# The 32x32 transposes of a block inverse as products with the identity: TensorE and ScalarE in place of VectorE

## The chip, the cores and the metric

The kernel runs on one core of one Trainium2 chip. The metric is the device time of one execution in microseconds. Three executions of the kernel before took 1997.05, 2003.13 and 1999.79 us; their median is 1999.79 us.

## The reference

A model on 256 tokens and 256 context tokens of width 1024, in several blocks: a first mixer that puts differential attention and an RWKV recurrence in both directions side by side, a state-space mixer, a second stack of attention kinds, each followed by a feed-forward part. Blocks are scaled and shifted by modulation vectors, products of a conditioning vector with large weights. Only the first mixer matters here, and in it two pieces:

```
def wkv_scan(r, decay, k, v, kk, b, s0, reverse):
    def step(s, inp):
        r_t, w_t, k_t, v_t, kk_t, b_t = inp
        sa = jnp.einsum('bhvk,bhk->bhv', s, -kk_t)
        s = s * w_t[:, :, None, :] + sa[..., None] * b_t[:, :, None, :] + v_t[..., None] * k_t[:, :, None, :]
        return s, jnp.einsum('bhvk,bhk->bhv', s, r_t)
    s, ys = lax.scan(step, s0, xs, reverse=reverse)
...
def diff_combine(s, lam, v):
    p = jax.nn.softmax(s.astype(jnp.float32), axis=-1)
    w = p[:, :, 0] - lam * p[:, :, 1]
    return jnp.einsum('bhqk,bhkd->bhqd', w.astype(v.dtype), v)
```

The kernel computes the scan in chunks of 64 tokens, eight in all. Since `sa` of a token depends on the tokens before it in its chunk, each chunk needs the inverse of a unit lower triangular 64x64 matrix, for each of eight heads and two directions. Four chunks are inverted together, 64 matrices in one call, and there are two calls.

## The kernel before

The program is written for one core as a class, `Kern`. Every step is a Python generator that yields its estimated cost; `weave` always advances the stream that has the smallest share of its own total done, and so fixes the order in which instructions are written down. A scheduler then orders them on each engine by priority and readiness; each engine executes its own list in that order.

The stretch of interest, about 180 to 500 us, weaves three streams. `rwkv_units` is the recurrence: preparation of the chunk matrices (L1022, L1025), `inverse` for the first half of the chunks, four `unit_step`s, `inverse` for the second half, four more. `dense` is the attention (`diff_head`: scores at L938, maximum at L941, exponentials at L944, two scalings on VectorE at L947 and L948, transposes at L952, values at L958) with its projections (L457), then, once the first half's units are done, the group norm (square roots at L563 to L573 on VectorE, statistics at L1290, gate L1311, output L1318) with modulation products between (`adas`, L483, whose weights `raw<-adaw` come in by SyncE's queue into 4 buffers), and last `out_early`, the output projection's first blocks (L1349). Its weights, too, are brought by SyncE's queue; ScalarE splits them into a high part `whi` (L424) and VectorE computes the low part `wlo` (L425). The third stream, `mods`, is more modulation products. ScalarE issues the DMAs that place the context's columns (L1336, L1337).

`inverse` keeps 32 matrices for each of four partition groups g of 32: two directions, and two diagonal blocks. In `LN` a partition is a matrix's row. The inversion wants one matrix per partition, so four transposes on VectorE (L1133) turn `LN` into `L`. Then 31 steps of two VectorE operations (L1141, L1143) build the inverse `Xi`. Six more transposes turn it back: two into `ta` (L1149), four into `LN` (L1150). 64 products per round at L1157 and L1167 with copies at L1160 (VectorE) and L1170 (ScalarE) fill the off-diagonal block. The products write to PSUM tiles of the tag `ya`, of which there are two; so do the y products of the units (L1081, L1108).

Of the kernel before, what the change touches and what calls it, by code (L numbers as in the profile page):

```python
# [10 lines left out]
AF = mybir.ActivationFunctionType  # L11
# [3 lines left out]
MUL, ADD, SUB, MAX, MIN = ALU.mult, ALU.add, ALU.subtract, ALU.max, ALU.min  # L15
# [287 lines left out]
class Kern:  # L303
# [599 lines left out]
    def diff_head(self, h, q, k, v, state):  # L903
        nc, P = self.nc, self.DF
        ident = self.C('ident')
        rot = []
        shuf = list(range(16, 32)) + list(range(16))
        for i, x in enumerate((q, k)):
            r = self.tl(P, [128, T], f'rot{i}')
            t = self.tl(P, [128, T], 'rott')  # L910
# [14 lines left out]
        for lat in range(2):  # L925
            nk = 2 + 2 * lat
            wT = self.tl(P, [128, 4, T], 'wT')
            for qt in range(2):
# [17 lines left out]
                nc.vector.reciprocal(st[:, 6:8], st[:, 4:6])  # L946
                nc.vector.tensor_scalar(e[:, 1], e[:, 1], st[:, 7:8], self.nlam, op0=MUL, op1=MUL)  # L947
                nc.vector.scalar_tensor_tensor(e[:, 0], e[:, 0], st[:, 6:7], e[:, 1], op0=MUL, op1=ADD)  # L948
# [107 lines left out]
    def unit_step(self, s, px, S):  # L1056
# [53 lines left out]
        for d in range(2):  # L1110
            c = sl if d == 0 else 3 - sl
            o = self.y[s // 4][:, :, 64 * c:64 * c + 64]
            src = py.rearrange("p (j d) c -> p j d c", d=2)[:, :, d]
            if d:
                src = src[:, :, ::-1]
            if sl < 2:
                nc.vector.tensor_copy(o, src)
            else:
                nc.vector.tensor_tensor(o, src, o, ADD)
# [3 lines left out]
    def inverse(self):  # L1123
# [4 lines left out]
        G4 = [slice(32 * g, 32 * g + 32) for g in range(4)]  # L1128
        lt = [self.LN[:, d].rearrange("p j h s c -> p (j h s) c") for d in range(2)]
        L = self.tl(U, [128, 32, 32], 'L')  # L1130
        for g in range(4):
            b = 32 * (g % 2)
            nc.vector.transpose(L[G4[g]], lt[g // 2][G4[g], :, b:b + 32].rearrange("p m t -> p t m"))  # L1133
        Xi = self.tl(U, [128, 32, 32], 'Xi')
        nc.gpsimd.memset(Xi, 0.0)
        nc.gpsimd.memset(Xi.rearrange("p a b -> p (a b)")[:, 0:1024:33], 1.0)
        yield 4.0
        for i in range(31):
# [6 lines left out]
        ta = self.tl(U, [128, 32, 32], 'L')  # L1145
        for g in (0, 2, 1, 3):
            b = 32 * (g % 2)
            if not g % 2:
                nc.vector.transpose(ta[G4[g]].rearrange("p m j -> p j m"), Xi[G4[g]].rearrange("p t j -> p j t"))  # L1149
            nc.vector.transpose(lt[g // 2][G4[g], :, b:b + 32].rearrange("p m t -> p t m"), Xi[G4[g]])  # L1150
            yield 1.5
        for half in range(2):
# [1193 lines left out]
```

## Time and profile before

| | |
|---|---|
| time, median of three | 1999.79 us |
| the profiled execution's time | 1991.42 us |
| its span, first to last instruction | 1989.6 us |
| TensorE busy | 1889.9 us, 95% |
| VectorE busy | 1445.1 us, 73% |
| ScalarE busy | 966.6 us, 49% |
| mean granted TensorE clock | 0.981 |

The profile shows one execution. PE is TensorE, DVE VectorE, ACT ScalarE, POOL GpSimd. A timeline row gives start and duration in us, engine, line, operation, output<-inputs with their shapes, a count where neighbours are drawn together, and in brackets the idle time of the engine just ahead of it with what ended it. Each float32 product leaves two records, so x128 is 64 products. PEclk is the granted clock as a share of full speed. A duration is that of the profiled execution; only the total has three runs.

### The profile page before, as it was taken

What the parts mean: (1) busy time and instruction counts of PE and PEld (TensorE: products, weight loads), DVE (VectorE), ACT (ScalarE), POOL (GpSimd) and SP (SyncE); (2) the same over time, 40 slices, a digit from 0 to 9 for tenths busy, and PEclk for the clock granted to TensorE, in tenths of its full rate; (3) what the DMA queues carried; (4) which work ended last, traced back from release to release, by engine and by line L of the source; (5) the groups of instructions that cost most, each with busy time, mean ns of one, the idle gap of its engine ahead of it and who ended that gap; (6) DMA issues with size and microseconds to landing.
All of it is one profiled execution on the core that took longest, in us unless ns stands there. A gap on an engine that the chain in (4) does not pass through costs nothing.

```text
span 1989.6 us, 37077 instructions
## 1 busy us (share of the span) xinstructions
PE 1889.9 (95%) x14690; PEld 1627.2 (82%) x14690; DVE 1445.1 (73%) x3032; ACT 966.6 (49%) x1772; POOL 220.8 (11%) x341
## 2 busy tenths in 40 slices
PE   5999889979899899998999999999999999999999
PEld 3776667647798889986778888899997888999999
DVE  3775696784799854447988888666678667778984
ACT  4455233222552434344565556456674554556653
POOL 2122402201231200011000002100030000000000
PEclk8999899979999999999999999999999999999999
DMA  7355724543388843332222224456654434356664
GB/s 297 111 187 184 233 75 128 170 138 108 116 282 241 281 169 96 96 99 74 86 74 81 83 82 144 147 180 181 186 165 155 145 106 128 119 167 183 193 191 147
DMA packets 87019, 299.78 MB, mean 151 GB/s; under 512 B 11213, under 2 KB 14685, under 8 KB 86846
## 3 DMA queue, kind: packets, MB, share of 16 engines
q1 hardware_dynamic: 62064, 221.29, 35.6%
q0 software_dynamic: 20736, 69.64, 10.7%
q10 hardware_dynamic: 4046, 6.49, 1.0%
q8 instruction: 115, 1.88, 0.4%
q14 instruction: 58, 0.48, 0.1%
HBM read 281.63 MB, written 18.90 MB: 151 GB/s over the span
## 4 chain that ended last, share of the span: by engine, by line
PE 82%; DVE 6%; DMA 4%; issue 4%; ACT 2%; POOL 1%; POOLq 0%; DVEq 0%; SPq 0%; ACTq 0%
PE psmm L457 22%; PE psmm L432 11%; PE psmm L435 11%; PE psmm L433 11%; PE psy L1752 2%; PE psmm L1689 2%; PE psmm L1349 2%; DMA ar<-adat 1%; PE psw L1757 1%; DVE wlo L425 1%; PE psa L2076 1%; PE psa L435 1%; PE psa L432 1%; PE psa L433 1%; PE pso L2125 1%
## 5 line engine op out<-in xcount | busy, mean ns | idle before, releaser
L424 ACT ACTIVATE whi<-raw 128x1024 fp32r<-128x1024 f32 x374 | 394.7, 1056 | 467.9 <-PE psmm L433 241.9
L425 DVE TENSOR_TENSOR wlo<-raw,whi 128x1024 fp32r<-128x1024 f32 x374 | 453.6, 1214 | 63.3 <-ACT whi L424 35.6
L457 PE MATMUL psmm<-hhi,whi 128*128 128x256 f32 (+1 forms) x1024 | 325.1, 340 | 6.2 <-ACT whi L424 2.5
L457 PE MATMUL psmm<-hlo,whi 128*128 128x256 f32 (+1 forms) x1024 | 319.3, 334 | 1.3 <-DVE hlo L708 1.3
L432 PE MATMUL psmm<-hhi,whi 128*128 128x258 f32 (+1 forms) x944 | 230.9, 283 | 0.5 <-ACT whi L424 0.5
L433 PE MATMUL psmm<-hlo,whi 128*128 128x258 f32 (+1 forms) x944 | 230.8, 282 | 0.0
L457 PEld LDWEIGHTS psmm<-hhi,whi 128*128 128x128 f32 x1024 | 195.0, 191 | 33.9 <-issue 10.3
L457 PEld LDWEIGHTS psmm<-hlo,whi 128*128 128x128 f32 x1024 | 195.0, 190 | 22.7 <-issue 4.2
L457 PE MATMUL psmm<-hhi,wlo 128*128 128x256 f32 (+1 forms) x1024 | 208.9, 335 | 0.3 <-DVE wlo L425 0.2
L432 PEld LDWEIGHTS psmm<-hhi,whi 128*128 128x128 f32 x944 | 178.9, 190 | 2.7 <-issue 1.0
L433 PEld LDWEIGHTS psmm<-hlo,whi 128*128 128x128 f32 x944 | 179.3, 190 | 0.7 <-issue 0.6
L457 PEld LDWEIGHTS psmm<-hhi,wlo 128*128 128x128 f32 x1024 | 154.1, 189 | 22.1 <-issue 6.6
L432 PE MATMUL psmm<-hi,whi 128*128 128x512 f32 (+1 forms) x512 | 162.4, 337 | 6.2 <-ACT hi L711 6.2
L433 PE MATMUL psmm<-lo,whi 128*128 128x512 f32 (+1 forms) x512 | 161.3, 336 | 0.0
L435 PE MATMUL psmm<-hhi,wlo 128*128 128x258 f32 (+1 forms) x944 | 132.3, 282 | 0.0
L435 PEld LDWEIGHTS psmm<-hhi,wlo 128*128 128x128 f32 x944 | 121.1, 190 | 0.0
L432 PEld LDWEIGHTS psmm<-hi,whi 128*128 128x128 f32 x512 | 96.4, 189 | 17.6 <-ACT hi L711 7.7
L521 DVE SCALAR_TENSOR_TENSOR aj<-ar,cb 128x1024 f32<-128x1024 f32 x80 | 97.6, 1220 | 13.0 <-DMA ar<-adat 10.7
L433 PEld LDWEIGHTS psmm<-lo,whi 128*128 128x128 f32 x512 | 96.4, 189 | 10.3 <-DVE lo L712 0.2
L435 PE MATMUL psmm<-hi,wlo 128*128 128x512 f32 (+1 forms) x512 | 100.1, 338 | 0.0
L1429 ACT ACTIVATE r<-r,s 128x256 f32<-128x256 f32 x96 | 48.9, 510 | 86.5 <-DVE r L1428 86.1
L435 PEld LDWEIGHTS psmm<-hi,wlo 128*128 128x128 f32 x512 | 81.5, 190 | 10.5
(607 smaller groups left out, 3681.1 us busy)
## 6 DMA issues: line engine op xcount, KB each, us to landing
raw<-w SPq DMA_DIRECT2D x128, 512.0 KB, 3.6
ar<-adat POOLq DMA_DIRECT2D x56, 512.0 KB, 5.0
raw<-win SPq DMA_DIRECT2D x55, 512.0 KB, 3.5
raw<-ssdin SPq DMA_DIRECT2D x49, 512.0 KB, 3.5
raw<-hyin SPq DMA_DIRECT2D x26, 512.0 KB, 5.4
raw<-adaw SPq DMA_DIRECT2D x24, 512.0 KB, 3.9
raw<-wg SPq DMA_DIRECT2D x22, 512.0 KB, 4.2
raw<-wu SPq DMA_DIRECT2D x22, 512.0 KB, 4.3
```

The lines of the kernel that those rows point to most:

```text
L424: nc.scalar.activation(hi[:, :n], raw, AF.Copy)
L425: nc.vector.tensor_tensor(lo[:, :n], raw, hi[:, :n].bitcast(F32), SUB)
L432: nc.tensor.matmul(ps, whi[:, k], act.hi[k][:, n0:n1], start=start and i == 0, stop=False)
L433: nc.tensor.matmul(ps, whi[:, k], act.lo[k][:, n0:n1], start=False, stop=False)
L435: nc.tensor.matmul(ps, wlo[:, k], act.hi[k][:, n0:n1], start=False, stop=stop and i == len(ks) - 1)
L457: nc.tensor.matmul(ps, w[:, k], a[k][:, n0:n1], start=i == 0, stop=i == len(runs) - 1)
L521: nc.vector.scalar_tensor_tensor(junk, raw, 1.0, cb[j], op0=MUL, op1=MUL, accum_out=self.mod[l][:, b, j:j + 1])
L1349: nc.tensor.matmul(ps[:, :n], w[:, c + k], a[k], start=c + i == 0, stop=c > 0 and i == len(runs) - 1, skip_group_check=True)
L1429: nc.scalar.activation(r[:, s], r[:, s], AF.Relu, bias=sh)
L1689: nc.tensor.matmul(ps, w[:, k0 + k], a[k], start=start and i == 0, stop=stop and i == len(runs) - 1, skip_group_check=True)
L1752: nc.tensor.matmul(o, w[:, q], m[:, q], start=d == 0 and n == 2 and q < 2 and k == 0, stop=k == 1 and d == 1 and n == 3, skip_group_check= ...
L1757: nc.tensor.matmul(ph, Bt[:, i], xw.rearrange("p h c -> p (h c)"), start=n != 1, stop=n > 0)
```

## The change

Three edits. The ten VectorE transposes of each inverse go; in their place `turned` makes 16 matrix columns at a time on TensorE: for each column and each partition group a 32x32 product, with the data as stationary operand and a 32x32 block of the identity moving, into a `ya` tile, which ScalarE copies to where the transpose had written. `turned` is used three times per inverse: for L (four groups, 128 products), `upper` (groups 0 and 2, 64) and `diagonal` (four groups, 128). Second, the scaling of the second softmax becomes a small VectorE product of 128x1 and a copy with scale on ScalarE. Third, the y copies of the first two units of a half go from VectorE to ScalarE. The estimated costs that the generators yield sum to the same.

```diff
--- before.py
+++ after.py
@@ -944,7 +944,8 @@
                     nc.scalar.activation(e[:, m], pss[m], AF.Exp, scale=0.125, bias=st[:, 2 + m:3 + m],
                                          accum_out=st[:, 4 + m:5 + m])
                 nc.vector.reciprocal(st[:, 6:8], st[:, 4:6])
-                nc.vector.tensor_scalar(e[:, 1], e[:, 1], st[:, 7:8], self.nlam, op0=MUL, op1=MUL)
+                nc.vector.tensor_tensor(st[:, 7:8], st[:, 7:8], self.nlam, MUL)
+                nc.scalar.activation(e[:, 1], e[:, 1], AF.Copy, scale=st[:, 7:8])
                 nc.vector.scalar_tensor_tensor(e[:, 0], e[:, 0], st[:, 6:7], e[:, 1], op0=MUL, op1=ADD)
                 yield 2.2
                 pt = self.PSt('w')
@@ -1114,7 +1115,7 @@
             if d:
                 src = src[:, :, ::-1]
             if sl < 2:
-                nc.vector.tensor_copy(o, src)
+                nc.scalar.activation(o, src, AF.Copy)
             else:
                 nc.vector.tensor_tensor(o, src, o, ADD)
         yield 0.8 * self.C_STEP
@@ -1127,14 +1128,25 @@
         nc, U = self.nc, self.U
         G4 = [slice(32 * g, 32 * g + 32) for g in range(4)]
         lt = [self.LN[:, d].rearrange("p j h s c -> p (j h s) c") for d in range(2)]
+        ident = self.C('ident')
+
+        def turned(out, rows, groups):
+
+            for i0 in (0, 16):
+                ps = self.PSt('ya').rearrange("p (i c) -> p i c", i=16)
+                for i in range(16):
+                    for g in groups:
+                        nc.tensor.matmul(ps[G4[g], i], rows(g, i0 + i), ident[G4[g], G4[g]], start=True, stop=True)
+                out(slice(i0, i0 + 16), ps)
+                yield 1.5
+
         L = self.tl(U, [128, 32, 32], 'L')
-        for g in range(4):
-            b = 32 * (g % 2)
-            nc.vector.transpose(L[G4[g]], lt[g // 2][G4[g], :, b:b + 32].rearrange("p m t -> p t m"))
+        yield from turned(lambda i, ps: nc.scalar.activation(L[:, i], ps, AF.Copy),
+                          lambda g, t: lt[g // 2][G4[g], :, 32 * (g % 2) + t], range(4))
         Xi = self.tl(U, [128, 32, 32], 'Xi')
         nc.gpsimd.memset(Xi, 0.0)
         nc.gpsimd.memset(Xi.rearrange("p a b -> p (a b)")[:, 0:1024:33], 1.0)
-        yield 4.0
+        yield 1.0
         for i in range(31):
             n, w = 31 - i, i + 1
             tmp = self.tl(U, [128, n, w], 'itmp', bufs=2)
@@ -1143,12 +1155,19 @@
             nc.vector.tensor_tensor(Xi[:, i + 1:, :w], Xi[:, i + 1:, :w], tmp, SUB)
             yield self.C_INV
         ta = self.tl(U, [128, 32, 32], 'L')
-        for g in (0, 2, 1, 3):
-            b = 32 * (g % 2)
-            if not g % 2:
-                nc.vector.transpose(ta[G4[g]].rearrange("p m j -> p j m"), Xi[G4[g]].rearrange("p t j -> p j t"))
-            nc.vector.transpose(lt[g // 2][G4[g], :, b:b + 32].rearrange("p m t -> p t m"), Xi[G4[g]])
-            yield 1.5
+
+        def upper(j, ps):
+            for g in (0, 2):
+                nc.scalar.activation(ta[G4[g], :, j], ps[G4[g]].rearrange("p j m -> p m j"), AF.Copy)
+
+        def diagonal(t, ps):
+            for g in range(4):
+                b = 32 * (g % 2)
+                nc.scalar.activation(lt[g // 2][G4[g], :, b + t.start:b + t.stop],
+                                     ps[G4[g]].rearrange("p t m -> p m t"), AF.Copy)
+
+        yield from turned(upper, lambda g, j: Xi[G4[g], :, j], (0, 2))
+        yield from turned(diagonal, lambda g, t: Xi[G4[g], t], range(4))
         for half in range(2):
             ms = slice(16 * half, 16 * half + 16)
             ps = self.PSt('ya').rearrange("p (m j) -> p m j", m=16)
```

In the listings below each row is an instruction (or neighbours alike, with their count) in TensorE's list: line, operation, output<-inputs with tile numbers, and the output's shape. Behind the change the lines have new numbers: L952, L958, L1051, L1066, L1077, L1157, L1167 and L1349 are L953, L959, L1052, L1067, L1078, L1176, L1186 and L1368; the products with the identity are L1139.

TensorE at the head of the second inverse, from the third modulation product (`psmm_3909`) on, before:

```order
L1051 MATMUL psx_4463<-uv_3599,LN_1971 64x64
L483 MATMUL psmm_3909<-raw_3914,scc_93 32x512
L1051 MATMUL psx_4463<-uv_3599,LN_1971 64x64 x6
L1066 MATMUL psx_4463<-S_2253,ar_3597 64x128 x8
L1077 MATMUL pss_4498<-S_2253,cst_83 64x512
L483 MATMUL psmm_3909<-raw_3916,scc_93 32x512
L483 MATMUL psmm_3909<-raw_3910,scc_93 32x512
L483 MATMUL psmm_3909<-raw_3912,scc_93 32x512
L483 MATMUL psmm_3909<-raw_3914,scc_93 32x512
L483 MATMUL psmm_3909<-raw_3916,scc_93 32x512
L1077 MATMUL pss_4498<-S_2253,cst_83 64x512
L952 MATMUL psw_3752<-cst_83,e_3720 128x128 x4
```

After the change, from the first product for L on (`psya`; `cst` is the identity), which stands behind the third modulation product and five key products (L1052):

```order
L1139 MATMUL psya_4151<-cst_83,LN_1971 32x32 x64
L1139 MATMUL psya_4217<-cst_83,LN_1971 32x32 x43
L953 MATMUL psw_4098<-cst_83,e_4065 128x128 x4
L1139 MATMUL psya_4217<-cst_83,LN_1971 32x32 x21
L483 MATMUL psmm_4383<-raw_4390,scc_93 32x512
L483 MATMUL psmm_4383<-raw_4384,scc_93 32x512
L959 MATMUL psw_4104<-wT_4005,vT_3880 128x256 x4
L483 MATMUL psmm_4383<-raw_4386,scc_93 32x512
L483 MATMUL psmm_4383<-raw_4388,scc_93 32x512
L483 MATMUL psmm_4383<-raw_4390,scc_93 32x512
L1052 MATMUL psx_5139<-uv_3943,LN_1971 64x64
L1067 MATMUL psx_5139<-S_2256,ar_3941 64x128 x8
```

The products for L have come in here, and the state products (L1066, now L1067) have moved from ahead of the last head's transposes (L952, now L953) to behind its values (L959).

TensorE after the last step of the first inverse, before:

```order
L483 MATMUL psmm_2884<-raw_2891,scc_93 32x512
L1157 MATMUL psya_2665<-L_2615,LN_1971 32x32
L1157 MATMUL psya_2717<-L_2615,LN_1971 32x32
L952 MATMUL psw_2600<-cst_83,e_2566 128x128 x4
L938 MATMUL psw_2620<-df_2359,df_2210 128x256
L938 MATMUL psw_2620<-rot_2441,rot_2435 128x256
L938 MATMUL psw_2621<-df_2359,df_2210 128x256
L938 MATMUL psw_2621<-rot_2441,rot_2435 128x256
L1157 MATMUL psya_2665<-L_2615,LN_1971 32x32 x31
L1157 MATMUL psya_2717<-L_2615,LN_1971 32x32 x31
L457 MATMUL psmm_3106<-hhi_109,whi_3102 128x512
```

After the change, behind 57 of the `upper` products (`psya_2751`, `psya_2803`), which follow the same four L483 rows:

```order
L953 MATMUL psw_2735<-cst_83,e_2700 128x128 x4
L938 MATMUL psw_2788<-df_2491,df_2213 128x256
L938 MATMUL psw_2788<-rot_2573,rot_2567 128x256
L938 MATMUL psw_2789<-df_2491,df_2213 128x256
L938 MATMUL psw_2789<-rot_2573,rot_2567 128x256
L1139 MATMUL psya_2803<-cst_83,Xi_2415 32x32 x7
L1139 MATMUL psya_2846<-cst_83,Xi_2415 32x32 x64
L1139 MATMUL psya_2921<-cst_83,Xi_2415 32x32 x64
L1052 MATMUL psx_3235<-uv_2260,LN_1971 64x64 x6
L953 MATMUL psw_2915<-cst_83,e_2786 128x128 x4
L1052 MATMUL psx_3235<-uv_2260,LN_1971 64x64 x2
L1176 MATMUL psya_3003<-L_2750,LN_1971 32x32 x32
```

The projection products (L457) that followed L1157 directly now come after the whole inverse; between the diagonal products (`psya_2846`, `psya_2921`) and L1176 stand key products and four transposes.

TensorE in the tail of the second inverse, before, where the first two L1157 products stand ahead of the output projection:

```order
L491 MATMUL psw_4044<-cst_83,adas_4042 128x128 x4
L1157 MATMUL psya_4275<-L_4223,LN_1971 32x32
L1157 MATMUL psya_4331<-L_4223,LN_1971 32x32
L1349 MATMUL psmm_4114<-hhi_4051,whi_4110 128x512
L1349 MATMUL psmm_4114<-hlo_4052,whi_4110 128x512
```

The `upper` products now stand at this place. The diagonal ones come three output blocks later, after the change:

```order
L1368 MATMUL psmm_4788<-hlo_4533,whi_4784 128x512
L1368 MATMUL psmm_4788<-hhi_4536,whi_4784 128x512
L1368 MATMUL psmm_4788<-hlo_4537,whi_4784 128x512
L1139 MATMUL psya_4795<-cst_83,Xi_4316 32x32 x64
L1368 MATMUL psmm_4788<-hhi_4543,whi_4784 128x512
L1368 MATMUL psmm_4788<-hlo_4544,whi_4784 128x512
L1368 MATMUL psmm_4788<-hhi_4525,wlo_4785 128x512
L1368 MATMUL psmm_4788<-hhi_4532,wlo_4785 128x512
L1368 MATMUL psmm_4788<-hhi_4536,wlo_4785 128x512
L1368 MATMUL psmm_4788<-hhi_4543,wlo_4785 128x512
L1139 MATMUL psya_4870<-cst_83,Xi_4316 32x32 x64
```

Both sets of 64 have come between the products of one output block.

## Rows read from the trace of the kernel before

**Rows 1.** The page, parts 1 and 4: span, engines' busy time, the chain.
```profile
span 1989.6 us, 37077 instructions
...
PE 1889.9 (95%) x14690; PEld 1627.2 (82%) x14690; DVE 1445.1 (73%) x3032; ACT 966.6 (49%) x1772; POOL 220.8 (11%) x341
...
PE 82%; DVE 6%; DMA 4%; issue 4%; ACT 2%; POOL 1%; POOLq 0%; DVEq 0%; SPq 0%; ACTq 0%
```

**Rows 2.** Busy us of each engine by stretch; PEclk, DMA share, GB/s.
```profile
240.00:250.00 10.00, 10.00 (x44) 7.89 (x44) 9.90 (x11) 1.66 (x2) 0.00 (x0) 1.00 0.26 77
280.00:290.00 10.00, 6.38 (x36) 3.97 (x34) 9.55 (x18) 2.10 (x6) 0.00 (x0) 0.96 0.43 152
290.00:300.00 10.00, 10.00 (x143) 8.22 (x143) 9.75 (x11) 3.87 (x7) 0.75 (x1) 0.53 0.17 64
320.00:380.00 60.00, 59.64 (x754) 45.28 (x753) 38.41 (x91) 18.93 (x47) 18.29 (x25) 1.00 0.46 135
440.00:450.00 10.00, 9.92 (x55) 8.44 (x54) 9.83 (x11) 2.12 (x2) 0.00 (x0) 1.00 0.29 72
```

**Rows 3.** Groups of instructions by line, 180 to 500 us: busy, mean ns, idle.
```profile
L944 ACT ACTIVATE e<-psw,st 128x256 f32<-128x256 f32 (+1 forms) x32 | 18.3, 576 | 40.9 <-DVE st L942 40.9
...
L1133 DVE STREAM_TRANSPOSE L<-LN 32x1024 f32<-32x1024 f32 x8 | 15.7, 1962 | 0.2
L1150 DVE STREAM_TRANSPOSE LN<-Xi 32x1024 f32<-32x1024 f32 x8 | 15.6, 1950 | 0.1
...
L1149 DVE STREAM_TRANSPOSE L<-Xi 32x1024 f32<-32x1024 f32 x4 | 8.1, 2034 | 0.1
L947 DVE TENSOR_SCALAR e<-e,st,lam 128x256 f32<-128x256 f32 (+1 forms) x16 | 8.1, 504 | 0.2
...
L1170 ACT ACTIVATE LN<-psya 32x512 f32<-32x512 f32 x8 | 4.7, 587 | 7.3 <-PE psya L1167 7.1
```

**Rows 4.** Timeline of PE, first inverse: start, us, instruction, idle before.
```profile
253.33 0.63 PE L952 MATMUL psw<-cst,e 128*128 128x128 f32 x4 [2.80 <-DVE e L948]
...
285.79 0.31 PE L1157 MATMUL psya<-L,LN 32*32 32x32 f32 x4 [1.10 <-DVE L L1149]
288.62 0.63 PE L952 MATMUL psw<-cst,e 128*128 128x128 f32 x4 [2.53 <-DVE e L948]
...
292.00 3.62 PE L1157 MATMUL psya<-L,LN 32*32 32x32 f32 x124
295.54 0.80 PE L457 MATMUL psmm<-hhi,whi 128*128 128x512 f32 x1
...
299.12 0.54 PE L457 MATMUL psmm<-hhi,whi 128*128 128x512 f32 x1
...
300.90 0.40 PE L457 MATMUL psmm<-hlo,whi 128*128 128x512 f32 x1
```

**Rows 5.** Timeline of PE around the second inverse.
```profile
386.39 1.05 PE L483 MATMUL psmm<-raw,scc 128*32 128x512 f32 x2 [0.36 <-DMA raw<-adaw]
...
389.89 1.90 PE L483 MATMUL psmm<-raw,scc 128*32 128x512 f32 x10
...
431.79 0.42 PE L1157 MATMUL psya<-L,LN 32*32 32x32 f32 x4 [4.92 <-DVE L L1149]
432.67 0.79 PE L1349 MATMUL psmm<-hhi,whi 128*128 128x512 f32 x1 [0.46 <-ACT whi L424]
...
459.77 2.21 PE L1167 MATMUL psya<-LN,L 32*32 32x32 f32 x128
```

**Rows 6.** Timeline of DVE around the second inverse's beginning.
```profile
384.31 1.90 DVE L1133 STREAM_TRANSPOSE L<-LN 32x1024 f32<-32x1024 f32 x1
...
393.63 0.20 DVE L1141 TENSOR_TENSOR itmp<-L,Xi 128x31 f32<-128x31 f32 x1
...
398.44 0.16 DVE L563 TENSOR_SCALAR rqv<-psw 128x4 f32<-128x4 f32 x1 [0.52 <-PE psw L552]
```

**Rows 7.** Timeline of ACT before the output projection's first split.
```profile
431.56 2.00 ACT L424 ACTIVATE whi<-raw 128x1024 fp32r<-128x1024 f32 x2 [5.39 <-DMA hhi<-xT]
```

## The prediction

> **What bounds the kernel now.** I read the page first: TensorE is busy for 95% of the span and carries 82% of the chain that ended last, VectorE 73% and 6%, ScalarE 49% and 2% [rows 1]. So VectorE time that is taken away is worth something only where TensorE waits for VectorE, and every product added where TensorE is full is paid in whole. Which places are which, a table of ten-microsecond stretches over the two inverses tells [rows 2]: from 320 to 380 us TensorE is busy for 59.64 of 60 us at full clock, around 440 us for 9.92 of 10. Between 280 and 300 it is different. It is busy for only 6.38 of 10 us, and in the next ten the granted clock is 0.53, about the lower of the two levels (1.2 of 2.4 GHz). That clock follows a stretch in which the engine waited.
>
> The timeline of TensorE names the waits. Around the first inverse they are 2.80 us at 253.33 (for the softmax's last scaling on VectorE), 1.10 us at 285.79 and 2.53 us at 288.62 [rows 4]; in all three VectorE is late because 2 us transposes stand in its queue. Around the second inverse the four first transposes end near 393.6 and the 31 steps begin [rows 6], while TensorE takes modulation products as their weights arrive (0.36 us of waiting for a DMA at 386.39); at the end it waits 4.92 us for a transposed quadrant at 431.79, but the output projection's first product can't start before 432.67 anyway, since it waits for a ScalarE weight split [rows 5], and that split for the DMAs of the context's columns [rows 7].
>
> **The change, part by part.** *What goes.* Per inverse VectorE loses four transposes of 1.96 us, two of 2.03 and four of 1.95 [rows 3]: 4 x 1.96 + 2 x 2.03 + 4 x 1.95 = 19.7 us. *What comes.* Per inverse 128 + 64 + 128 = 320 products of 32x32 with the identity, 640 in all, and ScalarE gets 2 copies of 128x512 and 12 of 32x512 (0.587 us each by the eviction at L1170, 12 of them 7.0 us [rows 3]).
>
> *The price of a product.* The nearest row is L1167 in the second inverse: 128 records, two for each float32 product, in 2.21 us at full clock, so 34.5 ns for a product when two of the 32x32 quadrants alternate [rows 5]. The `upper` set has the same two quadrants: 64 x 35 = 2.2 us. The other two sets go round four quadrants. If four work at once as two do, a product costs half, 17.5 ns; the modulation products, which go to four column groups of one PSUM tile, speak for it: one alone shows 1.05 us, but ten records, five products, 1.90 us [rows 5]. If the issue of instructions or the PSUM tile is the limit, it stays 35 ns. I take 24, nearer to the row that shows four at once: 128 x 24 = 3.1 us for each set, and 2.2 + 3.1 + 3.1 = 8.4 us per inverse, with bounds 2.2 + 256 x 17.5 = 6.7 and 2.2 + 256 x 35 = 11.2.
>
> The row of the modulation products writes four column groups from full-height weights, so it doesn't show four row groups in one tile. The Trainium skill, "TensorEngine Tiling (Array Packing)", Gotcha 1 (PSUM Pressure), says that different row tiles can't access the same PSUM bank at the same time; all four quadrants here write one tile. By that rule it would be 35 ns or more and the sum that of the queued quadrants below.
>
> *First inverse.* To be had: the waits 2.80 + 1.10 + 2.53 = 6.4 us, and the low clock. At that clock 124 records took 3.62 us, 58 ns a product, 1.5 us above 62 x 34.5 ns; eight projection products from 295.54 took 3.58 us, where the next seven took 1.78 (2.0 for eight) [rows 4], another 1.5; with the rotary and transposing products before them about 4 us. Together 10.4. To be paid: 8.4 us of products, since TensorE has no gap left once the waits are gone: 240 to 250, where the products for L fall, and 320 to 380 are full [rows 2]. And new waits: the order of the changed program puts the whole tail of this inverse ahead of the projection products, with little between. From the first diagonal product to L1176 there are 64 products (1.5 us) and eight copies one after the other on ScalarE (4.7 us); beside these TensorE has the other 64 products (1.5), the key products and four transposes (about 1.0): 6.2 - 2.5 = 3.7, of which I count 2.5, since the copies of the first half start while its products still run. 8.4 + 2.5 - 10.4 = **+0.5 us**.
>
> *Second inverse, head.* The 128 products stand behind the third modulation product, which waits for its weights until 386.39 and ends at 387.4 [rows 5]; with five key products behind it they start near 387.9. 3.1 us of products, 0.55 of a softmax transpose in between and a last copy of 0.6 let the steps start at 392.1 to 392.3 instead of 393.63. That 1.3 us is worth little: the steps share VectorE with a chain that begins with the last head's square roots (398.44 [rows 6]) and runs over the group norm to the weight split. That chain's TensorE rows now stand behind 3.1 us of products, and get back the moved state products (L1066 and one L1077, about 2 us): **+1.0 us**.
>
> *Second inverse, tail.* The 4.92 us wait for the transpose goes, but the split at 431.56 ends last there, not the transpose, so its `upper` products fall into a gap: nothing. TensorE busier in the gap could lift the clock of the first eight output products; they run at 0.43 us spacing up to 435.8, and half of their excess of 1.7 us is **-0.8**. The diagonal products, 3.1 us, lie between output products in a stretch that is full (9.92 of 10 [rows 2]); VectorE's relief is worth nothing there: **+3.1**.
>
> *Softmax scale and y copies.* On VectorE 0.504 us becomes a 128x1 product (about 0.15), and ScalarE adds about 0.58 (as its exponential [rows 3]): the chain of one chunk gets 0.2 longer, sixteen times, but TensorE waits for that chain three times in the stretch [rows 4], and two of these waits go: **+0.2**. The y copies change engines with TensorE at other units' products: 0. If that cover failed, eight times the difference of two engines' copies is under 1 us.
>
> Sum: 0.5 + 1.0 - 0.8 + 3.1 + 0.2 = **+4.0 us**. The profiled execution took 1991.42 us, so it would take 1995.4; that execution lies 8.4 us below the median of the runs, 1999.79, and the same change on the median gives **2003.8 us**.
>
> Bounds: the product's price moves the sum by -3.5 (17.5 ns in both inverses, `upper` unchanged) or +5.6 (35 ns); new waits 0 to 5, so 2.5 either way; the first inverse's clock, if not regained, +4; the clock of the output products 0 to 1.7, so 0.9 either way.
>
> **The rivals.** *Faster.* Four quadrants work at once, the copies hide, and the steps start early because weights for the modulation products come sooner (they are requested when buffers come free, and everything ahead ran earlier). Then -3.5 for the price, -2.5 for the waits, -0.9 for the clock, and the head's products start at 384.3, when the last evacuation of L1025 ends and the first transpose began [rows 6], instead of 387.9: -3.6. 4.0 - 10.5 = -6.5, **1993.3 us**. For it: the 1.90 us row. Against: that the copies hide needs fillers that the order doesn't have. It decides in my favour only if diagonal products cost under 20 ns and L1176 waits under 1 us.
>
> *Slower: quadrants queue.* Every product costs 35 ns, whatever its quadrant: 4.0 + 5.6 = +9.6, **2009.4 us**. For it: L1167 already has two quadrants and yet 34.5 ns, so the instructions, not the array, may be its limit; 640 products of two records and two weight loads each are many instructions. It decides from about 28 ns on.
>
> *Slower: the strided weights.* 256 of the products for L load a stationary operand with 512 bytes between its elements, 128 of `upper` 128 bytes; no row shows such a load. If they cost two ordinary products, 70 ns, L's sets grow by 5.9 us each and `upper`'s by 2.2: +16 us, **2020 us**. Against it: weight loads lie beside products on their own queue. The Trainium skill, "SBUF — State Buffer", Specifications (TRN2), states 16-byte cachelines that want two hits each for full bandwidth; every element here is on a line of its own, and no run here shows the cost.
>
> **How the numbers follow.** Chances: my forecast 0.48, the fast case 0.20, queued quadrants 0.24, strided weights 0.08. My forecast's own range is 1997 to 2010. The range for 8 in 10 reaches from the middle of the fast case to well past that of the queued quadrants: **1993 to 2014**; left out are half of the fast case, the strided weights and an edge of the queued ones. A measurement of this kernel tells about 0.3%, 6 us, from no change. Faster by more: 0.12 of the fast case and 0.05 of mine, 0.17. Slower by more: 0.08, 0.19 of the queued ones and 0.11 of mine, 0.38. Between: 0.45.
>
> **What would show it.** In the changed profile: L1139 at 15 to 28 ns a product in the four-quadrant sets and 35 in `upper`; the waits at L953 near 253 and 288 gone, and a new one of 1 to 4 us at L1176 for ScalarE; clock 1.00 around 290; the first step of the second inverse at 1 to 2 us before its place now; output products beginning within 2 us of their old distance from the modulation products; TensorE full from there on with the diagonal products in it. I am wrong if the tail of the first inverse stands still longer than its old waits together (6.4 us), if the strided sets cost twice the others, or if the group norm's chain, not the products, carries the difference.

## The result and the profile after

The changed kernel took 2015.55 us (median of 5; 2009.12 to 2017.38), the kernel before 1998.06 us (median of 5): ratio 1.0073, 95% interval [1.0052, 1.0093], 10 to 19 us slower (the two medians lie 17.5 us apart). On the prediction's base of 1999.79 us that is 2014.4 us: at the upper edge of the range for 8 in 10, 0.4 us above it, and past the forecast's own range (to 2010), on the slower side that had 0.38. The direction of the sum was right, its size of 4.0 us was not.

The page of the changed kernel, the parts of [rows 1]:

```profile
span 2014.2 us, 39681 instructions
...
PE 1917.7 (95%) x15970; PEld 1653.6 (82%) x15970; DVE 1401.1 (70%) x3004; ACT 994.2 (49%) x1824; POOL 220.7 (11%) x341
...
PE 78%; DVE 8%; issue 4%; DMA 3%; ACT 2%; POOL 2%; ACTq 0%; POOLq 0%; DVEq 0%; SPq 0%
```

VectorE lost 44 us of busy time and TensorE gained 28. The chain has moved from TensorE to waits on VectorE and others (82% to 78%).

Busy time by stretch, columns as in [rows 2]; the last row is the second inverse's tail:

```profile
280.00:290.00 10.00, 10.00 (x160) 7.50 (x159) 4.90 (x16) 4.32 (x9) 0.00 (x0) 1.00 0.01 2
290.00:300.00 10.00, 6.75 (x364) 5.78 (x361) 3.40 (x9) 8.52 (x16) 0.75 (x1) 0.97 0.10 31
320.00:380.00 60.00, 57.00 (x700) 43.06 (x698) 32.67 (x77) 23.00 (x53) 17.17 (x23) 1.00 0.55 173
440.00:450.00 10.00, 9.44 (x126) 8.20 (x122) 2.36 (x2) 4.24 (x6) 0.00 (x0) 0.52 0.79 282
460.00:470.00 10.00, 8.29 (x307) 6.96 (x307) 1.98 (x4) 5.69 (x9) 0.00 (x0) 0.83 0.19 58
```

The stretch at 280 us is full now, as predicted. But 290 to 300 has the gap instead (6.75 of 10), 320 to 380 is 57.00 of 60 instead of 59.64, and in the tail there is a gap in a stretch that was full, with the clock at 0.83. Over 440 to 450, where the first output products lie, the granted clock is 0.52, the lower level for nearly all of the ten us.

The copies of the diagonal blocks cost 587 ns each, as was taken from L1170. In the listings below "issue" is idle time for which the profile has no releaser.

Timeline of TensorE behind the first inverse's last step (compare [rows 4]); 283.93 are products of `upper`, 293.39 the second diagonal set, L1176 the old L1157:

```profile
283.93 3.48 PE L1139 MATMUL psya<-cst,Xi 32*32 32x32 f32 x114
...
293.39 1.16 PE L1139 MATMUL psya<-cst,Xi 32*32 32x32 f32 x114 [1.42 <-issue]
...
297.12 0.38 PE L953 MATMUL psw<-cst,e 128*128 128x128 f32 x2 [1.57 <-issue]
...
297.69 1.20 PE L1176 MATMUL psya<-L,LN 32*32 32x32 f32 x64
```

57 products of `upper` took 3.48 us, 61 ns each, at full clock. The wait for ScalarE that was expected ahead of L1176 is not there; two idle times without a releaser are, 1.42 and 1.57 us.

Around the second inverse (compare [rows 5]; 395.29 answers to 386.39, 443.57 to 432.67), and the first product of the stage that follows the recurrence (L432):

```profile
395.29 1.04 PE L483 MATMUL psmm<-raw,scc 128*32 128x512 f32 x2 [0.57 <-DMA raw<-adaw]
...
396.75 3.31 PE L1139 MATMUL psya<-cst,LN 32*32 32x32 f32 x214
...
401.41 0.69 PE L1139 MATMUL psya<-cst,LN 32*32 32x32 f32 x33 [0.48 <-issue]
...
439.17 3.84 PE L1139 MATMUL psya<-cst,Xi 32*32 32x32 f32 x128 [1.36 <-DVE Xi L1155]
443.57 0.80 PE L1368 MATMUL psmm<-hhi,whi 128*128 128x512 f32 x1 [0.56 <-ACT whi L424]
...
460.55 1.29 PE L1139 MATMUL psya<-cst,Xi 32*32 32x32 f32 x128
...
463.35 1.17 PE L1139 MATMUL psya<-cst,Xi 32*32 32x32 f32 x115
466.24 0.32 PE L1139 MATMUL psya<-cst,Xi 32*32 32x32 f32 x13 [1.71 <-issue]
...
528.56 0.74 PE L432 MATMUL psmm<-zhi,whi 128*128 128x256 f32 x4 [0.58 <-ACT zhi L711]
```

107 products for L took 3.31 us, 31 ns each; the 64 of `upper` at 439.17 took 3.84, 60 ns, at a granted clock of 0.53; the 64 diagonal ones at 460.55 took 1.29, 20 ns. In the second diagonal set TensorE stops for 1.71 us behind 57 products, again without a releaser. VectorE at the head (compare [rows 6]):

```profile
402.84 0.21 DVE L1153 TENSOR_TENSOR itmp<-L,Xi 128x31 f32<-128x31 f32 x1 [5.87 <-ACT L L1144]
...
409.99 0.16 DVE L563 TENSOR_SCALAR rqv<-psw 128x4 f32<-128x4 f32 x1 [1.66 <-PE psw L552]
```

Measured from the third modulation product, the first step is 0.3 us later than before (402.84 - 395.29 = 7.55 against 7.24), the square roots 2.65 later (14.70 against 12.05), the output projection's first product 2.0 later (48.28 against 46.28).

From here on four marks divide the time: the end of the chunk products L1022 ahead of the first inverse and ahead of the second, the output projection's first product, and L432. Of the kernel before, the rows of the first two marks and that of the last:

```profile
235.85 1.68 PE L1022 MATMUL psya<-Xi,bka 64*128 64x128 f32 x16 [0.68 <-DMA Xi<-ard]
...
381.99 1.05 PE L1022 MATMUL psya<-Xi,bka 64*128 64x128 f32 x10
...
510.94 0.74 PE L432 MATMUL psmm<-zhi,whi 128*128 128x256 f32 x4 [0.58 <-ACT zhi L711]
```

With [rows 5] the last stretch, the second inverse's tail with the units of the second half, is 510.94 - 432.67 = 78.3 us; after it is 528.56 - 443.57 = **85.0**. The marks of the first stretch after:

```profile
238.41 1.71 PE L1023 MATMUL psya<-Xi,bka 64*128 64x128 f32 x16
...
391.81 0.38 PE L1023 MATMUL psya<-Xi,bka 64*128 64x128 f32 x2
```

392.19 - 240.12 = 152.1 us. Before it was 145.5 (from 237.53 to 383.04). Three kernels below have the order of the kernel before up to here, second_only, no_back and head_second; they took 146.1, 147.1 and 147.3. The marks of second_only:

```profile
238.68 3.09 PE L1022 MATMUL psya<-Xi,bka 64*128 64x128 f32 x16
...
386.86 1.05 PE L1022 MATMUL psya<-Xi,bka 64*128 64x128 f32 x10
```

So against the mean of these four, 146.5, about 5.6 us of the loss lie in the first stretch, 1.8 between marks two and three (51.4 against 49.6) and 6.7 in the last: 14.1, which agrees with the ratio's 10 to 19. Each of these lengths is that of one execution.

How the first stretch is made up, for before, after and first_only (products in the first inverse alone, below), columns as in [rows 2]; beside after, what TensorE waited for ahead of the softmax's transposes there, columns as in [rows 3]:

```profile
237.53:383.04 145.51, 138.10 (x1487) 103.76 (x1486) 113.84 (x263) 46.40 (x105) 23.49 (x32) 0.96 0.35 109
```

```profile
240.12:392.19 152.07, 144.94 (x2127) 110.85 (x2128) 91.43 (x248) 62.90 (x135) 23.48 (x32) 0.98 0.34 105
...
L953 PE MATMUL psw<-cst,e 128*128 128x128 f32 x40 | 7.2, 286 | 3.0 <-issue 1.6 <-DVE e L949 1.3
```

```profile
239.73:390.99 151.26, 149.73 (x2128) 112.58 (x2128) 95.06 (x252) 54.28 (x119) 23.50 (x32) 0.93 0.34 106
```

TensorE stands idle for 145.51 - 138.10 = 7.4 us before and 152.07 - 144.94 = 7.1 us after, although the waits that the prediction named are gone; 3.7 us of the 7.1 are stops without a releaser. The mean granted clock is 0.96 before (0.95 in the three kernels with its order) and 0.98 after. In first_only it is the other way round, 1.5 us idle and a clock of 0.93, and the stretch is about as long.

### The profile page after: what moved, and what is told of

Its sections match the earlier page's. It is cut to its first block, busy times and chain, and to the rows that moved or that the text cites. A ratio compares the mean times of both kernels' runs of the same rounds, so it can differ in the third digit from the quotient of the medians.

```text
span 2014.2 us, 39681 instructions
## 1 busy us (share of the span) xinstructions
PE 1917.7 (95%) x15970; PEld 1653.6 (82%) x15970; DVE 1401.1 (70%) x3004; ACT 994.2 (49%) x1824; POOL 220.7 (11%) x341
## 4 chain that ended last, share of the span: by engine, by line
PE 78%; DVE 8%; issue 4%; DMA 3%; ACT 2%; POOL 2%; ACTq 0%; POOLq 0%; DVEq 0%; SPq 0%
PE psmm L457 22%; PE psmm L432 11%; PE psmm L435 11%; PE psmm L433 10%; PE psy L1771 2%; PE psmm L1368 2%; DVE aj L521 2%; PE psmm L1708 2%; DMA ar<-adat 2%; DVE wlo L425 1%; PE psw L1776 1%; PE psa L2095 1%; PE psa L435 1%; PE psa L432 1%; PE psa L433 1%
## 5 line engine op out<-in xcount | busy, mean ns | idle before, releaser
L457 PE MATMUL psmm<-hhi,whi 128*128 128x256 f32 (+1 forms) x1024 | 325.4, 340 | 7.6 <-ACT whi L424 3.9
L457 PE MATMUL psmm<-hlo,whi 128*128 128x256 f32 (+1 forms) x1024 | 319.8, 334 | 1.5 <-DVE hlo L708 1.5
L432 PE MATMUL psmm<-hhi,whi 128*128 128x258 f32 (+1 forms) x944 | 231.9, 283 | 0.5 <-ACT whi L424 0.5
L457 PEld LDWEIGHTS psmm<-hhi,whi 128*128 128x128 f32 x1024 | 195.3, 191 | 34.9 <-issue 9.8
L457 PEld LDWEIGHTS psmm<-hlo,whi 128*128 128x128 f32 x1024 | 195.7, 191 | 22.6 <-DVE hlo L708 4.2
L457 PE MATMUL psmm<-hhi,wlo 128*128 128x256 f32 (+1 forms) x1024 | 209.0, 334 | 0.3 <-DVE wlo L425 0.2
L432 PEld LDWEIGHTS psmm<-hhi,whi 128*128 128x128 f32 x944 | 178.7, 189 | 2.7 <-ACT whi L424 1.6
L457 PEld LDWEIGHTS psmm<-hhi,wlo 128*128 128x128 f32 x1024 | 153.8, 189 | 22.8 <-issue 7.3
L432 PE MATMUL psmm<-hi,whi 128*128 128x512 f32 (+1 forms) x512 | 163.0, 338 | 6.3 <-ACT hi L711 6.3
L432 PEld LDWEIGHTS psmm<-hi,whi 128*128 128x128 f32 x512 | 96.5, 189 | 17.8 <-ACT hi L711 8.0
```

The source lines that it names most:

```text
L432: nc.tensor.matmul(ps, whi[:, k], act.hi[k][:, n0:n1], start=start and i == 0, stop=False)
L457: nc.tensor.matmul(ps, w[:, k], a[k][:, n0:n1], start=i == 0, stop=i == len(runs) - 1)
```

## The experiments

All times are medians, and ratios to the kernel before with their 95% intervals. L and its lines are those of the change's diff.

**Which part?** Four kernels undo the change in pieces. `transposes_only` and `scales_only`:

```diff
# transposes_only: softmax scale and y copies as before
-                nc.scalar.activation(e[:, 1], e[:, 1], AF.Copy, scale=st[:, 7:8])
+                nc.vector.tensor_scalar(e[:, 1], e[:, 1], st[:, 7:8], self.nlam, op0=MUL, op1=MUL)
...
-                nc.scalar.activation(o, src, AF.Copy)
+                nc.vector.tensor_copy(o, src)
# scales_only: all transposes on VectorE, as before
```

> The products for the transposes alone; softmax scale and y copies stay on VectorE. Theory A (the transposes carry the whole loss, about 9 us at the first inverse and about 8.5 at the second): 14 to 18 us above the kernel before, as the full change. Theory B (the copies that went to ScalarE delay its queue and carry a good part of it): at most 10 us above.

> The softmax scale and the y copies on ScalarE alone, all transposes on VectorE. Theory A: within 3 us of the kernel before, and TensorE's waits around the inverses as in the kernel before. Theory B: 5 us or more above.

transposes_only: 2010.58 us, 1.0066 [1.0051, 1.0080], 10 to 16 us above. scales_only: 2001.93 us, 1.0030 [1.0016, 1.0044], 3 to 9 above. Neither theory holds alone: the transposes carry most, but the scales are not free, as theory A and the prediction (0.2) had them. The scales lengthen the first stretch to 151.0 us and transposes_only has 151.0 too, so in the full change's 152.1 the two don't add.

`first_only` and `second_only` have products in one of the two calls of `inverse` (with `st` handed in) and VectorE's transposes in the other:

```diff
-        yield from turned(lambda i, ps: nc.scalar.activation(L[:, i], ps, AF.Copy), ...
+        if (1, 0)[st]:          # second_only: (0, 1); likewise for upper and diagonal
+            yield from turned(lambda i, ps: nc.scalar.activation(L[:, i], ps, AF.Copy), ...
+        else:
+            for g in range(4):
+                nc.vector.transpose(L[G4[g]], ...
```

> Products for the transposes in the first inverse alone, everything else as before. Theory A: 6 to 10 us above the kernel before. The prediction's term for this inverse (+0.5): within 3 us. If the 4 us by which the changed kernel is late ahead of the first inverse come from DMAs that differ from run to run, about 4 us above.

> Products for the transposes in the second inverse alone. Theory A: 7 to 10 us above (2.4 at the head, 1.2 of low clock ahead of the output products, 5.5 in the tail). The prediction's term (+3.3): 3 to 4 us. Rival C, instruction loading: the idle times of TensorE that end with no releaser appear here too, 1.4 to 1.8 us behind about 57 diagonal products of a set, at the same count of instructions although the time is another.

first_only: 2006.60 us, 1.0044 [1.0028, 1.0059], 6 to 12 us above; its first stretch took 151.3 us, its last 80.0. second_only: 2006.92 us, 1.0058 [1.0041, 1.0075], 8 to 15 above. In second_only (TensorE; L1384 is the output product, L1138 the products with the identity):

```profile
437.05 0.80 PE L1384 MATMUL psmm<-hhi,whi 128*128 128x512 f32 x1 [8.29 <-ACT whi L424]
...
450.42 2.00 PE L1138 MATMUL psya<-cst,Xi 32*32 32x32 f32 x64
...
461.84 0.37 PE L1138 MATMUL psya<-cst,Xi 32*32 32x32 f32 x19 [0.43 <-issue]
...
522.65 0.73 PE L432 MATMUL psmm<-zhi,whi 128*128 128x256 f32 x4 [0.58 <-ACT zhi L711]
```

Its last stretch is 522.65 - 437.05 = 85.6 us, as long as in the full change, but made up otherwise. Rival C's stop has the expected place, behind 54 diagonal products, and not the expected size: 0.43 us instead of 1.4 to 1.8. In its stead all of `upper` (two groups of 32 products, 2.00 us each) lies between the output products here, where after it lies ahead of the first one; with 2.6 us of diagonal products that makes 7.0 of the 7.3 us above 78.3. Both inverses lose, each more than the prediction's +0.5 and +3.3. Here `upper` ran at full clock, and 32 of its products took 2.00 us: 62 ns, about the 60 at the low clock after.

**Is it the stride of the weights?** `weights_in_rows` is the full change with the stationary operands read along rows; it multiplies other elements than the inverse needs.

```diff
-                          lambda g, t: lt[g // 2][G4[g], :, 32 * (g % 2) + t], range(4))
+                          lambda g, t: lt[g // 2][G4[g], t, 32 * (g % 2):32 * (g % 2) + 32], range(4))
...
-        yield from turned(upper, lambda g, j: Xi[G4[g], :, j], (0, 2))
+        yield from turned(upper, lambda g, j: Xi[G4[g], j], (0, 2))
```

> The full change, but the stationary operands for L and upper are read along rows (32 neighbouring elements) instead of along columns (512 or 128 bytes apart): the same number of products, of other data, so the inverse it builds is not the one that is wanted. Theory A (a strided weight load is what makes L and upper dearer than diagonal): a product of the L sets falls from 32 to about 20 ns, of upper from 61 to about 35, 3.2 us less per inverse, and the whole is 3 to 6 us below the full change, 9 to 12 above the kernel before. Theory B (the sets differ by place or clock, not by stride): prices stay at 32 and 61 ns and the time stays within 2 us of the full change.

2007.33 us, 1.0040 [1.0025, 1.0054]: about 6 us below the full change. The products for L at the head of the second inverse:

```profile
387.63 1.19 PE L1139 MATMUL psya<-cst,LN 32*32 32x32 f32 x117
391.11 1.92 PE L1139 MATMUL psya<-cst,LN 32*32 32x32 f32 x128 [2.30 <-issue]
394.84 0.42 PE L1139 MATMUL psya<-cst,LN 32*32 32x32 f32 x11 [1.81 <-issue]
```

58 products in 1.19 us are 20 ns each, where the strided ones took 31: theory A. `upper` can't be compared, since without the column order its products started between the steps; so the total isn't the price of the stride alone. But the set as a whole is not quicker: TensorE now stops for 2.30 and 1.81 us without a releaser, and 128 products that need 2.6 us take 7.6. Something other than the array limits them.

**What are the stops?** Three kernels, all on the full change: each diagonal product of the second inverse twice; the diagonal products and their copies there left out; the sets written down in quarters.

```diff
# diag_twice (second inverse alone)
-        yield from turned(diagonal, lambda g, t: Xi[G4[g], t], range(4))
+        yield from turned(diagonal, lambda g, t: Xi[G4[g], t], [0, 1, 2, 3] * (1 + st))
# no_diag
+        if st == 0:
             yield from turned(diagonal, lambda g, t: Xi[G4[g], t], range(4))
+        else:
+            yield 3.0
# spread, in turned
+                    if i % 4 == 3 and i < 15:
+                        yield 0.375
                 out(slice(i0, i0 + 16), ps)
-                yield 1.5
+                yield 0.375
```

> The full change with each diagonal product of the second inverse issued twice (same result, 128 products more, no other instruction). If the array is the limit (20 ns a product): 2.6 us above the full change, the idle time without releaser behind 57 products still 1.7 us. If the supply of instructions is the limit (theory C): 4.5 us or more above, with two or three such idle times of 1.4 us or more instead of one.

> The full change without the diagonal products and their eight copies in the second inverse (left out; the second half's units work with the blocks as they were). The prediction's term for them, 3.1 us of products in a full stretch: 3 us below the full change. Theory A with the idle time counted in: 4.3 us below; with the low clock behind it too: 5.5 to 6 us.

> The full change, but the sets of products are written down in quarters, so that other products come between them (in the second tail 16, six output products, 48, and again). Theory C (supply of instructions): the idle time of 1.7 us in the second tail falls below 0.7 and the time by 1 to 2 us. If the idle time comes from the sets themselves (PSUM tiles, quadrants): it stays, and the time is within 1 us of the full change.

diag_twice: 2021.53 us, 1.0103 [1.0085, 1.0120]. TensorE, from the first output product to L432:

```profile
442.70 0.80 PE L1368 MATMUL psmm<-hhi,whi 128*128 128x512 f32 x1 [0.56 <-ACT whi L424]
...
458.55 2.29 PE L1139 MATMUL psya<-cst,Xi 32*32 32x32 f32 x249
464.56 0.33 PE L1139 MATMUL psya<-cst,Xi 32*32 32x32 f32 x7 [3.73 <-issue]
...
467.68 3.12 PE L1139 MATMUL psya<-cst,Xi 32*32 32x32 f32 x243
472.28 0.32 PE L1139 MATMUL psya<-cst,Xi 32*32 32x32 f32 x13 [1.48 <-issue]
...
535.90 0.74 PE L432 MATMUL psmm<-zhi,whi 128*128 128x256 f32 x4 [0.58 <-ACT zhi L711]
```

By the ratios it is 6 us above the full change, with intervals that overlap. The stretch is 93.2 us, 8.2 more than after: 128 products more at 64 ns each, although 249 records ran at 18 ns a product. The stops are 3.73 and 1.48 us where there was one of 1.71, and as in theory C they come after a certain number of instructions. The instruction queue's line of the page (packets, MB, share), before, after and here:

```profile
q8 instruction: 115, 1.88, 0.4%
```

```profile
q8 instruction: 125, 2.05, 0.4%
```

```profile
q8 instruction: 127, 2.08, 0.4%
```

After the change TensorE executes 2560 instructions more than before (1280 records and as many weight loads, by the page and [rows 1]), and 10 packets more came; the 512 of diag_twice (128 products with two records and two weight loads each) came with two: one packet of 16 KB for 256 instructions, 64 products. The 2 x 15970 instructions of TensorE after make 124.8 such packets, the 2 x 14690 before 114.8, so this queue is TensorE's. A set of 64 products is one packet, executed in 1.3 us.

no_diag (2011.31 us, 1.0051 [1.0034, 1.0068]):

```profile
447.13 0.80 PE L1371 MATMUL psmm<-hhi,whi 128*128 128x512 f32 x1 [1.08 <-ACT whi L424]
...
525.71 0.74 PE L432 MATMUL psmm<-zhi,whi 128*128 128x256 f32 x4 [0.58 <-ACT zhi L711]
```

78.6 us: without the diagonal sets the last stretch is as long as before. They cost 6.4 us there: 2.5 of products, the 1.71 us stop, and 1.7 of low clock behind the stop (0.83 over 460 to 470, in the table above) make 5.9. Its total lies only 4 us below the full change, with intervals that overlap; its profiled execution had a longer low clock in the first stretch.

spread (2014.75 us, 1.0071 [1.0051, 1.0092]):

```profile
443.69 0.80 PE L1370 MATMUL psmm<-hhi,whi 128*128 128x512 f32 x1
...
465.40 0.37 PE L1139 MATMUL psya<-cst,Xi 32*32 32x32 f32 x19 [1.11 <-issue]
...
526.94 0.74 PE L432 MATMUL psmm<-zhi,whi 128*128 128x256 f32 x4 [0.58 <-ACT zhi L711]
```

The stop shrinks to 1.11 us and the stretch to 83.3, 1.7 less, between both theories; the expected 0.7 us was not reached. The total can't tell it from the full change.

The trace also shows when each packet of this queue was taken and landed. Of the kernel after, the queue in the 1 us from 463.87 on:

```profile
q8 instruction: 1, 0.02, 5.8%
```

5.8% of 16 engines for 1 us are 0.92 us, so this packet landed at 464.79. TensorE had stopped at 464.5 and went on at 466.24. The same at other stops (us):

| kernel | TensorE stops | packet begins | lands | TensorE goes on | landing to going on |
|---|---|---|---|---|---|
| after | 292.0 | 290.92 | 291.95 | 293.39 | 1.44 |
| after | 464.5 | 463.87 | 464.79 | 466.24 | 1.45 |
| second_only | 461.4 | 459.44 | 460.38 | 461.84 | 1.46 |
| weights_in_rows | 388.8 | 388.73 | 389.83 | 391.11 | 1.28 |
| diag_twice | 460.8 | 462.32 | 463.28 | 464.56 | 1.28 |
| spread | 464.3 | 462.98 | 463.86 | 465.40 | 1.54 |

In all fourteen kernels together 36 stops of 0.2 us or more without a releaser lie between 240 and 560 us, and each ends 1.2 to 1.6 us behind the landing of such a packet. In the six rows the next packet begins 1.1 to 1.2 us after TensorE goes on, so where TensorE is held up in this way the packets follow each other at some 3.5 us (290.92 and 294.49 after, 388.73 and 392.28 in weights_in_rows), 55 ns for each of 64 products. The stop that ends at 297.12 after falls between two ordinary transposes (L953), so it isn't a matter of the small products' tiles. So theory C holds: the stops are waits for instructions. What takes the time between landing and going on, the trace doesn't tell.

**Is VectorE's relief worth anything?** `no_back` is the kernel before without the four transposes back into LN in the second inverse (`if st == 0` ahead of L1150).

> The kernel before without the four transposes that put the second inverse's result back into LN (left out; the units of the second half then work with the matrices as they were): 7.8 us of VectorE fewer in the tail of the second inverse. The prediction's claim that VectorE's relief is worth nothing there: within 2 us of the kernel before, and the stretch from the first output product to the end of the recurrence as long as before (78.3 us). If relief is worth something there, 3 to 8 us below.

1998.74 us, 0.9991 [0.9980, 1.0002]:

```profile
435.61 0.80 PE L1350 MATMUL psmm<-hhi,whi 128*128 128x512 f32 x1
...
514.02 0.74 PE L432 MATMUL psmm<-zhi,whi 128*128 128x256 f32 x4 [0.58 <-ACT zhi L711]
```

78.4 us, as before. The claim holds: 7.8 us of VectorE in that tail are worth nothing that can be measured.

**Is there a better half?** `head_second` has products for L in the second inverse alone, `diag_first` for the diagonal blocks of the first alone (flags as in first_only).

> The kernel before with products for L in the second inverse alone. Theory A (the second head's gain is given back): group norm begins about 4 us earlier, and the output projection's first product waits that much longer for its DMAs, so within 2 us of the kernel before. Rival: the head's products are what makes the second inverse slow: 3 us or more above. Third: 3 to 4 us below, if the loss on the way to the output projection came from the upper products.

> The kernel before with products for the diagonal blocks of the first inverse alone (contiguous weights, 20 ns each, 2.6 us), VectorE relieved of four transposes where TensorE waits for it. Theory A (TensorE's waits of 2.5 us there go, 2.6 us of products come): within 2 us of the kernel before. If the low clock at 290 to 300 us goes with the waits: 3 to 5 us below, faster than both kernels. If small products of themselves keep the clock low: 2 to 4 us above.

head_second: 2002.07 us, 1.0012 [1.0001, 1.0024]:

```profile
434.96 0.79 PE L1384 MATMUL psmm<-hhi,whi 128*128 128x512 f32 x1 [8.28 <-ACT whi L424]
...
517.24 0.74 PE L432 MATMUL psmm<-zhi,whi 128*128 128x256 f32 x4 [0.58 <-ACT zhi L711]
```

Counted from the second mark, the group norm's first statistics product begins 3.8 us earlier, and the first output product waits 8.28 us for the split, which itself waited 7.9 us for the DMAs; a part is given back there, and the rest in the tail (82.3 us), where the transposes that follow now stand ahead of VectorE's output work: at 454.87 TensorE waits 1.57 us for it (L1390). diag_first: 1998.86 us, 1.0002 [0.9989, 1.0014]: the waits that go and the products that come are even. Neither beats the kernel before.

**Which of the scales?** `softmax_only`: the softmax scale on ScalarE, all else before.

> The kernel before with the softmax scale alone on ScalarE (y copies and transposes on VectorE). The scales alone cost about 4 us where 0.2 was predicted. If the softmax scale is the cause (its chain from the exponential to the transposes is longer and the order around it is another): 3 to 5 us above the kernel before. If the y copies are: within 1.5 us.

2002.37 us, 1.0016 [1.0002, 1.0030]: 0.4 to 6 us above. It can be half of the scales' loss or all of it; whether the y copies have a share, the intervals don't tell. The last stretch is 78.3 us in both kernels, so the loss lies ahead of it. In scales_only it shows in the first stretch (151.0 against 146.5), in softmax_only more in the next (53.0 against 49.6), each in one execution; by what mechanism stays open.

## Why the prediction came out as it did

- *What bounds the kernel, and VectorE's relief: right.* The three waits around the first inverse, 6.4 us, are gone as such; all waits for the softmax's last scaling (L949) in the first stretch add up to 1.3 us. Relief in the full tail is worth nothing (no_back).
- *The price of a product: off, set by set.* I took 24, 35 and 24 ns for L, `upper` and diagonal; measured 31, 61 and 20. Per inverse 128 x 31 + 64 x 61 + 128 x 20 = 10.4 us instead of 8.4: 4 us of the missing 10. The four quadrants do work at once (20 against 34.5 ns [rows 5]), and the value for the contiguous set was near. The step that failed is "The `upper` set has the same two quadrants: 64 x 35": it took a row with contiguous operands as the price of strided ones. The strided rival, at 0.08, had the mechanism, 61 against 70 ns, where two quadrants load. (In the rival "faster", 512 products at 17.5 instead of 24 ns are 3.3 us, not 3.5.)
- *First inverse, +0.5: the term that failed most*, about 5.6 us instead of 0.7 with the scales, which by themselves lengthen this stretch too. The price of the products is 2 us of it. The clock came out as taken in this execution: 0.98 against 0.95 or 0.96 over some 150 us is 3 to 4.5 us by estimate, and about 4 were taken. What failed is "To be had: the waits": 2.5 us of new waits against the 6.4 that go would have left TensorE 3.9 us less idle, and it was 0.3 less (7.1 against 7.4). Stops for instructions took the place of the waits (3.7 us, two of them, 1.42 and 1.57, ahead of L1176), and not the wait for ScalarE; the rest are short waits for VectorE and ScalarE, most of them from 320 on (57.00 busy instead of 59.64). In first_only and transposes_only nearly all the waits do go (1.5 us idle in both), and there the clock is lost instead (0.93 in both): 151.3 and 151.0 us. What decides between the two stays open.
- *Second head, +1.0: too low.* The chain is late by 2.65 us and the output by 2.0. The steps begin 0.3 later instead of 1.3 earlier, since products for L cost 31 ns and a stop of 0.48.
- *Clock of the first output products, -0.8: the wrong way.* Before, they ran at the lower level until 435.8, 3.1 us; after, a clock of 0.52 over 440 to 450 means until about 449.6, 6 us. `upper` did fall into the gap, but began behind a wait of 1.36 us, and the low clock (0.53) was already there.
- *Second tail, +3.1: too low by half.* "3.1 us" counted products only (2.5 measured); the stop and the clock behind it make it 6.4.
- *Scales, +0.2: mis-sized*, 3 to 9 measured.
- *The rivals.* Queued quadrants gave 2009.4 by a wrong mechanism, since four don't queue; its remark that the instructions may be the limit is what diag_twice and the packets bear out, though by their supply and not by their issue. That the range reached to 2014 is owed to this rival, so that the time came out at its edge is luck, not a sum that was right.

The Trainium skill, "TensorEngine Tiling (Array Packing)", Gotcha 1 (PSUM Pressure), would have different row tiles never in one PSUM bank at the same time; 20 ns with four in one tile against 34.5 with two speaks against it here. The Trainium skill, "SBUF — State Buffer", Specifications (TRN2), states 16-byte cachelines that need at least two hits each for full bandwidth; 31 ns strided against 20 contiguous agrees.

## What to carry to other kernels

A transpose on an engine that nobody waits for costs nothing; as many small products on the bounding engine are paid in full, and more. Price small products by a row with the same operand layout, not only the same shape, and count the instructions: 64 products of 32x32 are 256 instructions, executed in 1.3 us, while packets of 256 never began less than 3.2 us apart in these runs. And ask of each relief which stretch it falls in: the same four transposes were worth about as much as the 2.6 us of products in one place (diag_first) and nothing in another (no_back).

## What was not expected of the hardware

- A weight load with 128 bytes between elements made a product cost 60 ns at the low clock and 62 at full clock; contiguous ones took 58 at the low clock [rows 4] and 34.5 at full [rows 5]. So the strided load isn't paced by TensorE's clock.
- TensorE's stream of dense small products runs out of instructions: it stops for 0.4 to 3.7 us in the rows shown, behind 54 to 64 products of a dense run or 121 to 125, and goes on 1.3 to 1.5 us after the next packet of 256 instructions has landed. The Trainium skill, "Runtime: NRT & Kernel Launch", Instruction fetch mechanics, says that fetching is hidden because instructions are dispatched more slowly than blocks of 256 arrive; at 20 ns for four instructions these stops speak against it.
- One execution can lie 6 us off its kernel's median: the profiled one of the kernel before took 1991.42 us against 1998.06. So stretches of single profiles differ too: second_only, whose order is the same up to there, ends its chunk products 4.9 us later than the kernel before (387.91 against 383.04), 4.2 of it ahead of the first inverse.
